# S5's tables in two buffer sets, a paced TensorE part and bias rows in pieces: one change to a four-layer hybrid kernel

## The chip, the cores and the metric

The kernel runs on one core of a Trainium2 chip. The metric is the device time of one execution in microseconds. A core has five engines that run side by side: TensorE (PE in the profile, with its weight loads as PEld), VectorE (DVE), ScalarE (ACT), GpSimd (POOL), and SyncE (SP), which here only issues DMA transfers. TensorE's clock has two levels, 1.2 and 2.4 GHz; the profile gives the granted clock of a stretch as a share of the higher one.

## The reference, cut to what matters

Four layers work on 256 tokens of width 1024 in float32. Each layer is half a SwiGLU FFN of width 2816, a mixer, and half an FFN again. The mixers are S5, HGRN2, gated DeltaNet and MoBA. The first layer's mixer, S5, holds 64 groups of 16 channels with 64 complex states each:

```
lam_bar = exp(lam * dt);  b_bar = ((lam_bar - 1) / lam) * (b_re + i b_im)
bu = einsum('blgh,gph->lbgp', u, b_bar)
h  = associative_scan: h[l] = lam_bar * h[l-1] + bu[l]
y  = real(einsum('lbgp,ghp->blgh', h, c)) + d_skip * u
x  = x + val * sigmoid(gate),   val, gate = split(gelu(y) @ w_glu)
```

The last layer's mixer, MoBA, is causal attention here (256 tokens are one block). A relative position bias of 32 buckets and 8 heads is added to its logits.

## The kernel before, in words

A FFN is worked off in units. A unit is two blocks of 128 rows of a weight matrix by 512 columns. For each unit SP loads the raw weights (L69, four raw buffers), ScalarE rounds them to a high part (L86), VectorE subtracts to get the low part (L87), and TensorE makes 12 matmuls of 128x512, three for each of two blocks and two token halves (L343 to L345). Four high and four low buffers let the split run four units ahead (`Weights.HL`). A FFN has 44 units of gate and up and then 22 of down. Every four units the hidden part h is transposed by TensorE (L435), then split too (L438, L439). After the last units the residual x is updated (L480) and transposed for the next stage (L226).

S5 needs tables that depend on its parameters alone: an inward table (`s5_in`), an outward table (`s5_out`), the kernel inside a chunk of eight tokens (`s5_k`), and powers of the rotation (`turn`, `s5_phases`). The generator `s5_prep` makes them beside the first FFN. It is advanced by `step`, which the FFN calls after each unit: at units 5, 7, ... 31, and then at each unit to 59. Its order is: loads of the parameters; transposes; exponentials and sines on VectorE; copies of lambda powers to `s5_l` (L667, GpSimd); scaling of b (L687 to L691); copies to `back` (L705, GpSimd); then a loop over eight j of eight groups each. In the loop GpSimd makes two halves of the inward table (L728 to L730) into a buffer `e`; VectorE makes the outward table (L733, L734, L736) into another part of `e`, which is stored (L737); TensorE multiplies for `s5_k` (L742, 16 matmuls); TensorE transposes the two inward halves (L756, 4 each), ScalarE copies each to one staging buffer `et` (L757), and SP stores it (L758). There is one `e`, so the steps of j+1 wait for those of j. After the loop GpSimd makes the first set of phases (L768 on).

The stage S5 itself loads the tables (L800, eight transfers for each `s5_k` part; L804 for the others) into five buffers in turn. Its order is: inward products (L862), VectorE's scan of the first half, the own-chunk products (L878 by `own`), outward transposes and products (L951, L878), then the same for the second half. In the second half's scan GpSimd makes one of two products of the first rotation (L894), which VectorE adds (L900); GpSimd makes before it the second set of phases and the eight products `xr` (L939). TensorE then does matmuls on zeros (L249) at three places.

The framework puts the instructions of an engine in an order of its own, by program order and by when they seem ready; it may move one forward past others. `keep_in_program_order` holds an instruction behind all that its engine was given before. An engine's queue is worked off in order, so one that waits holds all behind it.

The bias for MoBA is prepared in the second FFN (`moba_bias`): 26 small copies on GpSimd make a row for each head, and one transfer on ScalarE's queue writes each row 128 times to DRAM (L1713).

Of the kernel before, what the change touches and what calls it, by code (L numbers as in the profile page):

```python
# [9 lines left out]
F32 = mybir.dt.float32  # L10
# [16 lines left out]
def as_ap(ap, offset, dims):  # L27
    return bass.AP(tensor=ap.tensor, offset=ap.offset + offset, ap=dims)
# [71 lines left out]
class Model:  # L100
# [483 lines left out]
    def s5_prep(self, pool):  # L584


        nc, I = self.nc, self.I
# [131 lines left out]
        v.tensor_reduce(self.s5_place, self.ident.rearrange("p (a t) -> p t a", t=8), op=OP.add, axis=mybir.AxisListType.X)  # L719
        for j in range(8):  # L720
            r = slice(8 * j, 8 * j + 8)

            rs = (slice(8 * j, 8 * j + 4), slice(8 * j + 4, 8 * j + 8))
            for h, eb in zip(rs, ebs):
                wh = [128, 4, 8, 16]
                pb = [back[:, n, h].unsqueeze(3).to_broadcast(wh) for n in range(2)]
# [10 lines left out]
            dma(as_ap(self.s5_out, j * 1024, [[8192, 128], [128, 8], [1, 128]]), eo)  # L737

            p = self.aux.tile([128, 512], F32, name="aux")
            for g in range(2):  # L740
                for q in range(4):
                    nc.tensor.matmul(p[q * 32:q * 32 + 32, g * 128:g * 128 + 128],  # L742
                                     b1[:, 8 * j + 2 * q:8 * j + 2 * q + 2].rearrange("p g h -> p (g h)"),
                                     eo[:, 2 * q + g], start=True, stop=True)
# [8 lines left out]
            for h, eb in zip(rs, ebs):  # L753
                p = self.aux.tile([128, 512], F32, name="aux")
                for g in range(4):
                    nc.tensor.transpose(p[:, g * 128:g * 128 + 128], eb[:, g], self.ident)  # L756
                nc.scalar.copy(et.rearrange("p g c -> p (g c)"), p)  # L757
                dma(as_ap(self.s5_in, h.start * 128, [[8192, 128], [128, 4], [1, 128]]), et)  # L758

        self.s5_turn = pool.tile([128, 2, 16, 32], F32, name="s5turn", tag="s5pw")  # L760
        yield from self.s5_phases(self.s5_turn, 0, pool)

    def s5_phases(self, turn, half, pool):

        eng = self.nc.gpsimd
        t2 = pool.tile([128, 2, 16, 8], F32, name="s5t2", tag="s5F")
# [13 lines left out]

    def s5_token(self, k):

        self.nc.vector.transpose(self.s5_u[:, k].rearrange("p g t h -> p t g h"),
                                 self.s5_x[:, k].rearrange("p (c t) -> p t c", t=8))

    def s5(self, i):
        nc = self.nc
# [3 lines left out]
        tags = ["s5" + c for c in "ABCDE"]  # L791

        def load(kind, part):

            tags.append(tags.pop(0))
            t = self.s5_pool.tile([128, 16, 128], F32, name="tab", tag=tags[-1])
            if kind == "t":

                for s in range(8):
                    nc.sync.dma_start(t[s * 16:s * 16 + 16],  # L800
                                      as_ap(self.s5_k, part * 16 * 3840 + (7 - s) * 16, [[240, 16], [3840, 16], [1, 128]]))
            else:
                src = self.s5_in if kind == "in" else self.s5_out
                nc.sync.dma_start(t, as_ap(src, part * 2048, [[8192, 128], [128, 16], [1, 128]]))  # L804
            return t.rearrange("p (j q g) c -> p j q g c", q=4, g=2)
# [890 lines left out]
    def moba_bias(self, pool):  # L1696
# [16 lines left out]
        nc.scalar.dma_start(self.bias_rows, row.rearrange("h (o s) -> h o s", o=1).to_broadcast([8, 128, 384]))  # L1713

    def moba(self, i):
# [3 lines left out]
        with self.tc.tile_pool(name="moba", bufs=1) as pool, self.tc.tile_pool(name="moba2", bufs=2) as two:  # L1719
            bt = pool.tile([128, H, L], F32, name="bt")  # L1720
            if self.bias is not None:
                self.bias(pool)
# [96 lines left out]
```

## Time and profile before

| | us |
|---|---|
| median of 3 runs | 2225.79 (2224.76 to 2226.97) |
| the profiled execution: time, and span of its instructions | 2227.23, 2225.5 |
| TensorE matmul busy | 2142.0 (96%) |
| VectorE, ScalarE, GpSimd busy | 1452.5, 1159.0, 207.8 |
| granted TensorE clock, mean | 0.982 |

The profiled execution is one run under the hardware profiler; the difference of its time and its span is what lies around the program. Times within a trace count from the first instruction. Busy TensorE is no measure of useful work, as matmuls overlap and last longer at the lower clock. The first FFN ends near 245 us, S5 is from there to some 320 us, and the second FFN begins there.

### The profile page before, as it was taken

The numbers are of one execution on the slowest core, as the hardware profiler recorded it, in microseconds if no ns is written. First come the engines' busy times: TensorE is split into PE (matmuls) and PEld (weight loads), VectorE is DVE, ScalarE is ACT, GpSimd is POOL, SyncE is SP. The second block draws the span as 40 slices with busy tenths as digits, with TensorE's granted clock in tenths as the row PEclk, the third lists the DMA queues.
The fourth block names the chain that finished last, engine by engine and source line by source line (L and its number), as shares of the span: only waits on it lengthen the run. The fifth ranks groups of instructions, "written<-read, shape, count | busy, mean of one in ns | idle before, by whom it ended". The sixth has DMA issues, their size and how long they took to land.

```text
span 2225.5 us, 30259 instructions
## 1 busy us (share of the span) xinstructions
PE 2142.0 (96%) x11480; PEld 1768.3 (79%) x11480; DVE 1452.5 (65%) x2445; ACT 1159.0 (52%) x1876; POOL 207.8 (9%) x272
## 2 busy tenths in 40 slices
PE   8988888999999999999999999998999999999998
PEld 6766666888888888888788887787888888898886
DVE  7987674556555977555655788887555555666555
ACT  6434344445444855444544677764544544555443
POOL 0598600000000000001000000000000000000000
PEclk9999999999999999999999999999999999999999
DMA  8655966655555554655555543334555655655553
GB/s 252 191 193 200 250 184 161 205 175 191 186 189 190 171 168 136 189 178 189 176 180 176 163 141 105 105 115 131 175 186 180 199 182 187 199 162 170 189 180 105
DMA packets 317907, 389.64 MB, mean 175 GB/s; under 512 B 14192, under 2 KB 247856, under 8 KB 316736
## 3 DMA queue, kind: packets, MB, share of 16 engines
q1 hardware_dynamic: 314768, 383.92, 54.5%
q10 hardware_dynamic: 2800, 3.68, 0.9%
q8 instruction: 90, 1.47, 0.3%
q14 instruction: 57, 0.47, 0.1%
q0 software_dynamic: 192, 0.10, 0.0%
HBM read 375.65 MB, written 12.01 MB: 174 GB/s over the span
## 4 chain that ended last, share of the span: by engine, by line
PE 80%; ACT 5%; DVE 5%; issue 4%; DMA 3%; POOL 2%; SPq 0%; ACTq 0%; POOLq 0%; DVEq 0%
PE acc L343 23%; PE acc L345 23%; PE acc L344 23%; PE acc L311 2%; PE aux L435 2%; PE acc L312 2%; DVE lo L87 2%; PE acc L313 2%; ACT hi L86 1%; DMA raw<-in_ffn_w_up_dram 1%; ACT zb L1512 1%; PE aux L226 1%; POOL s5e L730 1%; POOL s5e L729 1%; POOL s5tmp L728 1%
## 5 line engine op out<-in xcount | busy, mean ns | idle before, releaser
L87 DVE TENSOR_TENSOR lo<-raw,hi 128x1024 fp32r<-128x1024 f32 x681 | 850.0, 1250 | 585.3 <-ACT hi L86 583.6
L86 ACT CAST hi<-raw 128x1024 fp32r<-128x1024 f32 x681 | 713.0, 1049 | 703.0 <-PE acc L345 648.0
L343 PE MATMUL acc<-hi,xhl 128*128 128x512 f32 x1568 | 625.7, 399 | 8.6 <-ACT hi L86 8.2
L344 PE MATMUL acc<-lo,xhl 128*128 128x512 f32 x1568 | 615.9, 393 | 2.4 <-DVE lo L87 2.3
L345 PE MATMUL acc<-hi,xhl 128*128 128x512 f32 x1568 | 615.3, 393 | 0.0
L343 PEld LDWEIGHTS acc<-hi,xhl 128*128 128x128 f32 x1568 | 296.1, 189 | 70.8 <-ACT hi L86 9.1
L345 PEld LDWEIGHTS acc<-hi,xhl 128*128 128x128 f32 x1568 | 296.0, 189 | 64.4 <-issue 0.9
L344 PEld LDWEIGHTS acc<-lo,xhl 128*128 128x128 f32 x1568 | 296.6, 189 | 63.6 <-DVE lo L87 5.1
L343 PE MATMUL acc<-hi,hhl 128*128 128x512 f32 x704 | 276.3, 392 | 0.0
L345 PE MATMUL acc<-hi,hhl 128*128 128x512 f32 x704 | 276.1, 392 | 0.0
L344 PE MATMUL acc<-lo,hhl 128*128 128x512 f32 x704 | 275.0, 391 | 0.0
L344 PEld LDWEIGHTS acc<-lo,hhl 128*128 128x128 f32 x704 | 132.5, 188 | 27.4
L345 PEld LDWEIGHTS acc<-hi,hhl 128*128 128x128 f32 x704 | 132.5, 188 | 27.4
L343 PEld LDWEIGHTS acc<-hi,hhl 128*128 128x128 f32 x704 | 132.6, 188 | 27.0
L313 PE MATMUL acc<-xhl,lo 128*128 128x256 f32 x520 | 150.0, 290 | 0.0
L311 PE MATMUL acc<-xhl,hi 128*128 128x256 f32 x520 | 149.7, 291 | 0.0
L312 PE MATMUL acc<-xhl,hi 128*128 128x256 f32 x520 | 148.4, 288 | 0.0
L423 ACT ACTIVATE sl<-acc,norm_r 128x256 f32<-128x256 f32 x176 | 83.6, 475 | 109.3 <-PE acc L345 88.6
L426 DVE TENSOR_TENSOR h<-acc,sl 128x256 f32<-128x256 f32 x176 | 74.0, 420 | 49.8 <-ACT sl L423 49.8
L313 PEld LDWEIGHTS acc<-xhl,lo 128*128 128x128 f32 x520 | 100.1, 193 | 2.0 <-DVE lo L87 1.0
L311 PEld LDWEIGHTS acc<-xhl,hi 128*128 128x128 f32 x520 | 99.7, 193 | 1.8 <-issue 0.9
L312 PEld LDWEIGHTS acc<-xhl,hi 128*128 128x128 f32 x520 | 99.9, 193 | 1.3 <-issue 1.1
(563 smaller groups left out, 2148.5 us busy)
## 6 DMA issues: line engine op xcount, KB each, us to landing
raw<-in_ffn_w_gate_dram SPq DMA_DIRECT2D x174, 512.0 KB, 3.8
raw<-in_ffn_w_up_dram SPq DMA_DIRECT2D x174, 512.0 KB, 4.8
raw<-in_ffn_w_down_dram SPq DMA_DIRECT2D x80, 1024.0 KB, 4.9
raw<-in_gdn_w_in_dram SPq DMA_DIRECT2D x24, 1024.0 KB, 5.2
raw<-in_hg_w_in_dram SPq DMA_DIRECT2D x16, 1024.0 KB, 5.4
raw<-in_moba_w_in_dram SPq DMA_DIRECT2D x12, 1024.0 KB, 5.1
raw<-in_ffn_w_down_dram SPq DMA_DIRECT2D x16, 512.0 KB, 3.7
raw<-in_s_w_glu_dram SPq DMA_DIRECT2D x16, 512.0 KB, 6.1
```

The source lines that it names most:

```text
L86: pin(self.nc.scalar.copy(hi, src))
L87: self.nc.vector.tensor_tensor(lo, src, hi.bitcast(F32), op=OP.subtract)
L226: nc.tensor.transpose(q[:, j * 128:j * 128 + 128], self.x[:, t, k * 128:k * 128 + 128], self.ident)
L311: t.matmul(p, hi, ah, start=first, stop=False)
L312: t.matmul(p, hi, al, start=False, stop=False)
L313: t.matmul(p, lo, ah, start=False, stop=last)
L343: mm(p, ah, hi[:, j], start=first and j == 0, stop=False)
L344: mm(p, ah, lo[:, j], start=False, stop=False)
L345: mm(p, al, hi[:, j], start=False, stop=last and j == n - 1)
L423: nc.scalar.activation(sl, p[:, :256], AF.Silu, scale=self.r_col[:, t:t + 1])
L426: return nc.vector.tensor_tensor(waiting[-1][1][:, t], p[:, 256:], sl, op=OP.mult)
L435: nc.tensor.transpose(q[:, c:c + 128], h[:, t, f * 128:f * 128 + 128], self.ident)
```

## The change

The table preparation gets a second buffer (`s5f`), so that j and j+1 write to different sets. TensorE's part of the loop is held in program order, and the transposes of j-1 (`turned`) come at the end of the turn of j. The generator is advanced at unit 2, at 6 to 9, at the even units to 18, and at each unit from 19 on; the loop takes 5 units for each of j = 0 to 3 and 4 for the others. The copies to `s5_l` and `back` go to ScalarE. At the end of the preparation, units 61 to 63, six tables are loaded, and the steps of the first phases stand between them; S5 has six table buffers for five. The bias rows are written by 32 transfers instead of one, one for each unit of the second FFN from unit 6 on.

```
             steps = [0]
+            bias = None
+            if self.prep is None and self.bias is not None:
+                bias = self.bias(pool)
+                self.bias = None
...
-                if self.prep is not None and n > 4:
-                    for _ in range(n % 2 if n < 32 else 1 if n < 60 else 0):
-                        next(self.prep, None)
+                if bias is not None and n > 4:
+                    next(bias, None)
+                if self.prep is not None and (n == 2 or 5 < n < 10 or n > 9 and n % 2 == 0 or n > 18):
+                    next(self.prep, None)
...
-            if self.prep is None and self.bias is not None:
-                self.bias(pool)
-                self.bias = None
...
-                    nc.gpsimd.tensor_copy(self.s5_l[q * 32:q * 32 + 32, n].rearrange("p (j g a) -> p j g a", j=8, g=2)[:, :, :, a],
+                    nc.scalar.copy(self.s5_l[q * 32:q * 32 + 32, n].rearrange("p (j g a) -> p j g a", j=8, g=2)[:, :, :, a],
...
-            nc.gpsimd.tensor_copy(back[:, :, :, n], pw[:, :, :, 8 - n])
+            nc.scalar.copy(back[:, :, :, n], pw[:, :, :, 8 - n])
         e = pool.tile([128, 16, 128], F32, name="s5e", tag="s5C")
-        eo, ebs = e[:, :8], (e[:, 8:12], e[:, 12:16])
+        more = pool.tile([128, 16, 128], F32, name="s5f", tag="s5G")
+        eos = e[:, :8], more[:, :8]
+        ebs = [(t[:, 8:12], t[:, 12:16]) for t in (e, more)]
...
+        pin = self.tc.keep_in_program_order
+        def turned(j):
+            for n, eb in enumerate(ebs[j % 2]):
+                p = self.aux.tile([128, 512], F32, name="aux")
+                for g in range(4):
+                    pin(nc.tensor.transpose(p[:, g * 128:g * 128 + 128], eb[:, g], self.ident))
+                nc.scalar.copy(et.rearrange("p g c -> p (g c)"), p)
+                dma(as_ap(self.s5_in, (8 * j + 4 * n) * 128, [[8192, 128], [128, 4], [1, 128]]), et)
...
             dma(as_ap(self.s5_out, j * 1024, [[8192, 128], [128, 8], [1, 128]]), eo)
+            yield
...
-                    nc.tensor.matmul(p[q * 32:q * 32 + 32, g * 128:g * 128 + 128],
+                    pin(nc.tensor.matmul(p[q * 32:q * 32 + 32, g * 128:g * 128 + 128],
...
             yield
-            for h, eb in zip(rs, ebs):
-                p = self.aux.tile([128, 512], F32, name="aux")
...
-                dma(as_ap(self.s5_in, h.start * 128, [[8192, 128], [128, 4], [1, 128]]), et)
+            if j < 4:
+                yield
+            if j:
+                turned(j - 1)
+            yield
+        turned(7)
+        self.s5_tags = ["s5" + c for c in "ABCDEG"]
+        self.s5_tabs = []
         self.s5_turn = pool.tile([128, 2, 16, 32], F32, name="s5turn", tag="s5pw")
-        yield from self.s5_phases(self.s5_turn, 0, pool)
+        phases = self.s5_phases(self.s5_turn, 0, pool)
+        for kind, part in (("in", 0), ("in", 1), ("in", 2), ("in", 3), ("t", 0), ("t", 1)):
+            self.s5_tabs.append(self.s5_load(kind, part))
+            next(phases, None)
+            if part % 2:
+                yield
...
-        nc.scalar.dma_start(self.bias_rows, row.rearrange("h (o s) -> h o s", o=1).to_broadcast([8, 128, 384]))
+        for k in range(0, 128, 4):
+            yield
+            self.tc.keep_in_program_order(nc.scalar.dma_start(
+                as_ap(self.bias_rows, k * 384, [[128 * 384, 8], [384, 4], [1, 384]]),
+                row.rearrange("h (o s) -> h o s", o=1).to_broadcast([8, 4, 384])))
```

`s5_load` is the former `load` of S5, with the six tags; S5's `load` takes the six tables from `s5_tabs` first and calls `s5_load` for the rest.

## Rows read from the trace of the kernel before

**Rows 1.** A stretch of the first FFN: length, busy us of each engine, clock, DMA.
```profile
114.00:172.80 58.80, 47.56 (x278) 36.43 (x277) 49.07 (x34) 21.95 (x34) 54.82 (x31) 0.91 0.56 192
```
**Rows 2.** Waits of TensorE to 330 us: total, times, longest.
```profile
PE acc L878 <- DMA tab<-s_k: 11.9, 3, 5.0
PE aux L756 <- POOL s5e L730: 11.2, 5, 3.5
PE aux L742 <- DVE s5e L736: 6.2, 3, 3.2
```
**Rows 3.** Timeline of TensorE, both FFNs: start us, duration us, instruction.
```profile
114.00 0.60 PE L435 MATMUL aux<-ident,h 128*128 128x128 f32 x4
...
120.03 0.64 PE L742 MATMUL aux<-s5e,s5D 128*32 128x128 f32 x16
...
123.50 1.04 PE L756 MATMUL aux<-ident,s5e 128*128 128x128 f32 x8
...
244.74 0.66 PE L226 MATMUL aux<-ident,x 128*128 128x128 f32 x4 [0.21 <-DVE x L480]
...
356.80 0.60 PE L435 MATMUL aux<-ident,h 128*128 128x128 f32 x4
...
368.18 0.60 PE L435 MATMUL aux<-ident,h 128*128 128x128 f32 x4
...
389.85 0.60 PE L435 MATMUL aux<-ident,h 128*128 128x128 f32 x4
```
**Rows 4.** The loop's three GpSimd lines: ns minimum, median, maximum; first and last start.
```profile
L728 POOL TENSOR_TENSOR s5tmp<-s5D,s5kk x16: 1058/1917/1925, 109.6 to 200.2; 128x512 f32<-128x512 f32 x16
...
L729 POOL TENSOR_TENSOR s5e<-s5D,s5kk x16: 1047/1916/2040, 110.6 to 195.9; 128x512 f32<-128x512 f32 x16
...
L730 POOL TENSOR_TENSOR s5e<-s5e,s5tmp x16: 1269/2140/2357, 113.7 to 202.2; 128x512 f32<-128x512 f32 x16
```
**Rows 5.** Groups of VectorE in 110 to 205 us: busy, mean ns, idle before.
```profile
L87 DVE TENSOR_TENSOR lo<-raw,hi 128x1024 fp32r<-128x1024 f32 x22 | 40.5, 1842 | 14.3 <-ACT hi L86 14.3
L734 DVE TENSOR_TENSOR s5e<-s5E,s5pw 128x1024 f32<-128x1024 f32 x7 | 12.8, 1829 | 1.0 <-DMA s_out<-s5e 0.8 <-PE aux L742 0.3
```
**Rows 6.** Timeline of VectorE before GpSimd's loop.
```profile
87.25 1.22 DVE L87 TENSOR_TENSOR lo<-raw,hi 128x1024 fp32r<-128x1024 f32 x1
```
**Rows 7.** Timeline of GpSimd.
```profile
86.00 12.20 POOL L667 COPY s5l<-s5small 32x16 f32<-32x16 f32 x16 [9.42 <-DVE s5small L510]
...
204.29 0.12 POOL L768 MEMSET s5turn<- 128x16 f32 x1
...
229.73 0.43 POOL L500 TENSOR_TENSOR s5turn<-s5t 128x112 f32<-128x112 f32 x1
243.99 0.13 POOL L768 MEMSET turn<- 128x16 f32 x1 [13.83 <-PE acc L345]
...
278.05 2.49 POOL L894 TENSOR_TENSOR tb<-inc,turn 128x512 f32<-128x512 f32 x2
```
**Rows 8.** Timelines of VectorE and TensorE at the end of S5's second scan.
```profile
280.57 1.29 DVE L900 TENSOR_TENSOR inc<-S,tb 128x512 f32<-128x512 f32 x2 [7.17 <-POOL tb L894]
...
288.03 1.31 DVE L948 STREAM_TRANSPOSE sc<-S 128x512 f32<-128x512 f32 x2
...
290.38 1.22 PE L951 MATMUL aux<-ident,sc 128*128 128x128 f32 x8
```
**Rows 9.** Issues of transfers: KB each, median us to landing.
```profile
s_in<-s5tmp SPq DMA_DIRECT2D x16, 256.0 KB, 3.8
```
**Rows 10.** Timeline of ScalarE and its queue in the second FFN.
```profile
348.66 0.79 ACTq L1713 DMA_DIRECT2D bias_rows<-row  x1
...
382.73 1.04 ACT L86 CAST hi<-raw 128x1024 fp32r<-128x1024 f32 x1 [15.60 <-DMA raw<-in_ffn_w_up_dram]
```
**Rows 11.** Two stretches of the second FFN, columns as in rows 1 (last: GB/s).
```profile
370.00:375.00 5.00, 5.00 (x23) 4.13 (x22) 0.00 (x0) 0.00 (x0) 0.00 (x0) 1.00 0.51 84
385.00:390.00 5.00, 4.91 (x13) 3.85 (x14) 3.89 (x7) 3.03 (x5) 0.00 (x0) 0.53 0.99 336
```

More of the change, by code (lines that the diff above doesn't have):

```diff
@@ L719, in s5_prep @@
         v.tensor_reduce(self.s5_place, self.ident.rearrange("p (a t) -> p t a", t=8), op=OP.add, axis=mybir.AxisListType.X)
+        pin = self.tc.keep_in_program_order
[6 more added lines that the diff above has]
+                dma(as_ap(self.s5_in, (8 * j + 4 * n) * 128, [[8192, 128], [128, 4], [1, 128]]), et)
         for j in range(8):
             r = slice(8 * j, 8 * j + 8)
-            rs = (slice(8 * j, 8 * j + 4), slice(8 * j + 4, 8 * j + 8))
-            for h, eb in zip(rs, ebs):
+            eo = eos[j % 2]
+            for n, eb in enumerate(ebs[j % 2]):
+                h = slice(8 * j + 4 * n, 8 * j + 4 * n + 4)
                 wh = [128, 4, 8, 16]
-                pb = [back[:, n, h].unsqueeze(3).to_broadcast(wh) for n in range(2)]
+                pb = [back[:, m, h].unsqueeze(3).to_broadcast(wh) for m in range(2)]
                 g = nc.gpsimd.tensor_tensor
@@ L741, in s5_prep @@
                 for q in range(4):
-                    nc.tensor.matmul(p[q * 32:q * 32 + 32, g * 128:g * 128 + 128],
-                                     b1[:, 8 * j + 2 * q:8 * j + 2 * q + 2].rearrange("p g h -> p (g h)"),
-                                     eo[:, 2 * q + g], start=True, stop=True)
+                    pin(nc.tensor.matmul(p[q * 32:q * 32 + 32, g * 128:g * 128 + 128],
+                                         b1[:, 8 * j + 2 * q:8 * j + 2 * q + 2].rearrange("p g h -> p (g h)"),
+                                         eo[:, 2 * q + g], start=True, stop=True))
             nc.scalar.copy(kk[:, j % 4].rearrange("p g c -> p (g c)"), p[:, :256])
@@ L752, in s5_prep @@
             yield
-            for h, eb in zip(rs, ebs):
-                p = self.aux.tile([128, 512], F32, name="aux")
-                for g in range(4):
-                    nc.tensor.transpose(p[:, g * 128:g * 128 + 128], eb[:, g], self.ident)
-                nc.scalar.copy(et.rearrange("p g c -> p (g c)"), p)
-                dma(as_ap(self.s5_in, h.start * 128, [[8192, 128], [128, 4], [1, 128]]), et)
-        self.s5_turn = pool.tile([128, 2, 16, 32], F32, name="s5turn", tag="s5pw")
-        yield from self.s5_phases(self.s5_turn, 0, pool)
+            if j < 4:
[6 more added lines that the diff above has]
+        self.s5_tabs = []
+        self.s5_turn = pool.tile([128, 2, 16, 32], F32, name="s5turn", tag="s5pw")
+        phases = self.s5_phases(self.s5_turn, 0, pool)
[4 more added lines that the diff above has]
+                yield
     def s5_phases(self, turn, half, pool):
         eng = self.nc.gpsimd
-        t2 = pool.tile([128, 2, 16, 8], F32, name="s5t2", tag="s5F")
+        t2 = self.s5_pool.tile([128, 2, 16, 8], F32, name="s5t2", tag="s5F")
         pin = self.tc.keep_in_program_order
@@ L779, in s5_phases, with s5_load @@
             yield
+    def s5_load(self, kind, part):
+        tags = self.s5_tags
+        tags.append(tags.pop(0))
+        t = self.s5_pool.tile([128, 16, 128], F32, name="tab", tag=tags[-1])
+        if kind == "t":
+            for s in range(8):
+                self.nc.sync.dma_start(t[s * 16:s * 16 + 16],
+                                       as_ap(self.s5_k, part * 16 * 3840 + (7 - s) * 16, [[240, 16], [3840, 16], [1, 128]]))
+        else:
+            src = self.s5_in if kind == "in" else self.s5_out
+            self.nc.sync.dma_start(t, as_ap(src, part * 2048, [[8192, 128], [128, 16], [1, 128]]))
+        return t.rearrange("p (j q g) c -> p j q g c", q=4, g=2)
     def s5_token(self, k):
@@ L790, in s5 @@
         pin = self.tc.keep_in_program_order
-        tags = ["s5" + c for c in "ABCDE"]
+        tags = self.s5_tags
         def load(kind, part):
[L795 to L805, printed above, removed]
+            if self.s5_tabs:
+                return self.s5_tabs.pop(0)
+            return self.s5_load(kind, part)
         with ExitStack() as ctx:
@@ L1721, in moba @@
             if self.bias is not None:
-                self.bias(pool)
+                self.settle(self.bias(pool))
             nc.scalar.dma_start(bt, as_ap(self.bias_rows, 127, [[383, 128], [128 * 384, H], [1, L]]))
```

## The prediction

> **What bounds the kernel now.** I read the table of stretches first, then TensorE's list of waits, then the timelines of the engines that these name. E below is the moment of the last transpose of the first FFN, 244.74 us [rows 3]. In 114.0 to 172.8 TensorE is busy for 47.56 of 58.80 us at a granted clock of 0.91, while GpSimd is busy for 54.82 [rows 1]: here the first FFN is held up by S5's table preparation, which runs beside it. The list of waits has three large items: the transposes of the inward table wait 11.2 us for GpSimd (L730), the small products (L742) 6.2 us for VectorE, and S5's own products 11.9 us for loads of its tables [rows 2].
>
> How much of that is on the path? Four units and one transposition of h take 368.18 - 356.80 = 11.38 us where nothing disturbs them [rows 3]; with 0.45 us for the transposition (an estimate, below its 0.60 because matmuls overlap), a unit is 2.73 us. After the transposition at 114.00, 33 of the 66 units are left. They need 33 x 2.73 = 90.1; three more transpositions 1.4; eight groups of L742 at 0.64 make 5.1; sixteen halves of L756 at 0.52 make 8.3; the turning of x about 1.2 [rows 3]. That is 106.1 us, and 130.7 pass. So 24.6 us are lost: 17.4 of them are the two waits, and the rest is the clock that falls behind them [rows 1, 2].
>
> The S5 stage is another matter. Its waits for tables look large, but the last step that releases the end of S5 is VectorE at L900, which waits 7.17 us for GpSimd (L894, begun at 278.05) [rows 7, 8]. VectorE ends its scan at 289.3, and TensorE transposes at 290.38: the late table costs about 1.1 us there, not 11.9.
>
> **The change part by part: the first FFN.** The preparation begins at unit 2 instead of 5. The loop over eight j begins at unit 25 instead of 34, with 5 units for each of j = 0 to 3 and 4 for the others. TensorE's part of j is pinned behind it: L742 two calls after j's VectorE part begins, the transposes of j-1 at the end of j's turn. GpSimd may start j when the transposes of j-2 have freed its buffer, and has until the end of the turn of j+1. Four units with L742 and two halves are 10.9 + 0.64 + 1.04 = 12.6 us. GpSimd's three instructions take per half 1.06 + 1.05 + 1.27 = 3.4 us at best and 1.92 + 1.92 + 2.14 = 6.0 at the median [rows 4], so 6.8 to 12.0 per j. Even the upper end is inside 12.6 and has most of a further turn to spare; only the last j has just the five units 57 to 61, 15.3 us. So both waits and the clock that falls with them should go: -24.6 us.
>
> What takes their place is VectorE. A low part (L87) takes 1.22 us without GpSimd beside it [rows 6], 1.84 on the mean in 110 to 205, where 42 such two-input operations and GpSimd's 48 stand together (22 of L87 and 20 of the three table operations, of which one row stands) [rows 5]. Undisturbed these would be 42 x 1.22 = 51 and 16 x 3.4 = 54, together 105 us of work in 95: the two overlap by a factor of at least 1.1. After the change, units 33 to 61 take TensorE 28 x 2.73 + 1.4 + 3.8 + 6.2 = 87.8 us. In them lie 28 low parts and about 18 table operations, 56 us, and six j of GpSimd, 41: 97 us. At a factor of 1.1 that just fits, one after the other it costs 9 us. Lower bound 0, upper 10; I take +5, the middle, since the four split buffers hold some of it.
> The Trainium skill, "SBUF — State Buffer", section "Who interferes with whom", speaks against this part: a VectorE operation with two SBUF inputs and a GpSimd operation that reads SBUF exclude each other for the whole instruction. By it these 97 us would stand in 87.8, and my sum would be 4 us longer. The measured 105 us in 95 say that it doesn't hold to the full here.
>
> **Copies on ScalarE.** The 24 copies of L667 leave GpSimd, where the last 16 take 12.2 us and hold everything behind them [rows 7], and 8 more at L705. So GpSimd's loop can start some 20 us sooner. No row shows such a copy on ScalarE. From below, 128 of the 1024 elements of its cast of 1.04 us [rows 10] make 0.13; from above, GpSimd's own 12.2 / 16 = 0.76. So 4 to 24 us, over some 11 units; I take 0.3, nearer the ScalarE row, 10 us. Even at 24 ScalarE would fall 10 us behind its casts, and the four split buffers hold 4 x 2.73 = 11. I cost the copies at nothing; without that cover it is up to 10 us. Each pair of inward transposes shares one staging buffer, so the second copy waits for the first's store, 3.8 us [rows 9]; the casts are queued behind it, and TensorE behind those after four units. In a turn of 12.6 us ScalarE then has four casts, 4.2, six operations of at most half a cast's elements, estimated at 0.6 each, 3.6, and this 3.8: 11.6, just covered. Uncovered it would be up to 4 us per j; I leave that to the second rival.
>
> **Six early loads and phases.** They move four one-piece loads and 16 small ones on SP from S5's stage to units 61 to 63, past S5's weight loads. SP can hold there until the last inward store has landed (2 x 3.8 us plus the copies); behind it stand weights for products some 50 us after E, so I cost this at nothing; without that cover it is 8 us. The first turn's phases move too. Before, GpSimd makes them from 204.29 to 230.16, long before E, and starts the second set at 243.99 [rows 7]. Now the first set stands behind j = 7, which waits for the transposes at unit 56. From there GpSimd needs 0.5 + 6.8 to 12.0 + 25.9 = 33.2 to 38.4 us; TensorE reaches E after 10 units, L742, two pairs of halves, the x turning and 0.8 us of evacuation: 27.3 + 0.6 + 2.1 + 1.2 + 0.8 = 32.0. So the second set starts 1.2 to 6.4 us after E, where it now starts 0.75 before. Behind it, as now, come the eight products for xr and then L894: 278.05 - 243.99 = 34.1 us [rows 7]. So the step that VectorE waits for at L900 comes 2.0 to 7.2 us later, measured from E; I take 4, the lower half, as GpSimd meets fewer VectorE operations late in the FFN. The tables are early now, which gives the 1.1 us. S5: +3, between +1 and +6.
>
> **Bias rows in 32 pieces.** One transfer of 1536 KB is issued at 348.66, and until ScalarE gets its weights again at 382.73, after 15.60 us of waiting [rows 10], 34 us pass. In 370 to 375 the core moves 84 GB/s, in 385 to 390 it moves 336 [rows 11]. From the transposition at 368.18 to the next, 389.85, 21.67 us pass instead of 11.38 [rows 3]: 10.3 us lost, the half clock afterwards in it. Thirty-two pieces, one a unit, are each 1/32 of these 34 us, so about 1.1 us in 2.73. At 84 GB/s for 1.1 us and 336 for 1.63 that is 234 GB/s on the mean, and a unit needs 0.52 MB in 2.73 us, 192: enough. ScalarE issues 32 times: the one issue was 0.79 us [rows 10], 0.3 to 0.8 each. A unit holds 1.04 for the cast and about 0.4 for the rest, below 2.73 in either case. Nothing. So -10.3; bounds -10.3 and 0.
> The Trainium skill, "DMA: Bandwidth & Descriptors", section "Bandwidth", speaks against pieces: transfers under 64 KB are dominated by their descriptors, and a MiB or more is advised. These are 48 KB. No one waits for them before the last layer, so by it too the sum would stay unless their packets cost the weights more than one transfer's do.
>
> **Sum.** -24.6 + 5 + 3 - 10.3 = -26.9 us. The profiled execution, span 2225.5 and time 2227.23, would be 2198.6 and 2200.3. The median of the runs is 1.4 below that time, 2225.79, so **2199 us**. A change under 0.2%, 4.5 us, can't be told from none.
>
> **Rivals.** (1) The forecast, 2193 to 2206: 0.58. (2) VectorE and GpSimd exclude each other, or the store wait reaches TensorE in one or two j: 10 instead of 5 in the FFN, GpSimd late by the full 6 in S5, some clock lost again, +3: -24.6 + 10 + 6 + 3 - 10.3 = -16, 2210. For it: VectorE at 49 of 58.8 us [rows 1]; against: the 105 in 95. 0.16. By the page on SBUF that is named above, the first half of this is the case. (3) Nothing is given back: the port fits, GpSimd is done by E, S5 gains the 1.1: -36, 2190. For it: 1.1 is what the trace shows; against: j = 7 can't start before unit 56. 0.15. (4) The pieces disturb the weights as the one did: -16.6, 2209; for it: 234 against 192 is no wide margin, and no row shows a piece. 0.05. (5) The other side: pinned, TensorE waits for GpSimd in every j, where now the scheduler's order may let a unit pass. It decides when a j takes over 12.6 us; to be slower by 0.2% it must lose 31 us in eight, a j of about 16.5. The median instructions give 12.0. 0.04. That the tables land earlier and change nothing is part of (1) already. The remaining 0.02 are for a loss that cancels the gain within 0.2%.
> The range 2187 to 2213 holds (1) to (4) with their bounds. Faster 0.94, same 0.02, slower 0.04.
>
> **What would show it.** Right: the L756 and L742 waits are gone from TensorE's list, the clock is at 1.00 from 114 to E, E falls at 220 to 230; transpositions of h stay 11.4 apart through the second FFN; ScalarE no longer waits 15 us there. S5's waits for tables are small, yet L900 still waits for GpSimd, and the time from E to the last pair of S5's outward transposes (290.38, now 45.6 us) is longer by 1 to 6 [rows 3, 8]. Wrong: TensorE waiting for L87 between units 33 and 61 by over 10 us; new PE waits behind L730; a shorter S5 stage, which would mean that GpSimd's phases were not last.

## The result, and the profile after

The changed kernel takes 2206.47 us (median of 4 runs, 2204.64 to 2208.11) against 2225.28 (2221.11 to 2226.97): ratio 0.9918, 95% interval 0.9901 to 0.9935, some 19 us faster. The forecast was 2199, with 2187 to 2213 as its range. So sign and range hold, but 19 us came where 27 were expected, and they came from other places than the sum says.

The profiled execution took 2208.11 us, its span is 2206.4. Beside the span of before, 2225.5, the 19.1 us split up as follows, by the same marks in both traces:
- until the last transposition of the first FFN (E): 239.28 instead of 244.74, -5.5 us;
- from E to the first transposition of h in the second FFN: 112.21 instead of 112.06, +0.15; in it S5, from E to its last pair of outward transposes, 46.62 instead of 45.64, +1.0;
- from there to the first transposition of h in the third FFN: 187.25 instead of 197.29, -10.0: the bias;
- all behind that: 1667.7 instead of 1671.4, -3.7. No edit works there. Below, a kernel whose instructions differ from the changed one's only in a buffer of S5's loop shows 1664.2 there, so this is difference from run to run.

The marks in the traces, first of the changed kernel (E, the second FFN, the third), then of the kernel before (the third):

```profile
239.28 0.63 PE L226 MATMUL aux<-ident,x 128*128 128x128 f32 x4 [1.04 <-ACT size L865]
...
351.49 0.60 PE L435 MATMUL aux<-ident,h 128*128 128x128 f32 x4
...
538.74 0.60 PE L435 MATMUL aux<-ident,h 128*128 128x128 f32 x4
```
```profile
554.09 0.60 PE L435 MATMUL aux<-ident,h 128*128 128x128 f32 x4
```

Of the signs that the prediction named, the waits of L756 and L742 are gone and so is ScalarE's wait of 15 us. Three others failed: E is not at 220 to 230, the clock is at 0.82 from 94.64 to 131.7 instead of 1.00 from 114 on, and S5's waits for tables are as large as before.

TensorE's waits up to 330 us, of the changed kernel (total, times, longest), answer to [rows 2]; L731 is the line of the inward transposes now, L759 that of the small products, L908 that of S5's own products:

```profile
PE aux L435 <- DVE h L426: 13.5, 6, 4.3
PE acc L908 <- DMA tab<-s_k: 12.2, 3, 6.4
```

L756's and L742's waits, 17.4 us together, are gone. In their place stands a wait that was 1.4 us before: the transposition of h (L435) waits 13.5 us for VectorE. Three stretches say where. The first row is of the kernel before, the others of the changed kernel (length, busy us of PE, PEld, DVE, ACT, POOL, clock, DMA share, GB/s):

```profile
78.00:114.00 36.00, 34.54 (x156) 28.25 (x157) 30.99 (x43) 16.96 (x22) 27.14 (x30) 1.00 0.62 191
```
```profile
78.00:131.70 53.70, 41.17 (x194) 32.03 (x192) 47.75 (x45) 23.21 (x49) 31.56 (x15) 0.87 0.47 154
131.70:239.30 107.60, 106.49 (x588) 85.77 (x587) 74.23 (x64) 54.56 (x86) 80.59 (x91) 1.00 0.71 234
```

From the transposition at unit 21 to that at unit 33, 35.9 us passed before (78.1 to 114.0), and 52.9 pass now (78.84 to 131.7). From unit 33 to E the new kernel is all but perfect: 107.6 us where the prediction worked out 106.1 for the bare work, TensorE busy for 106.49, the clock at 1.00. Before, that part took 130.7. So the removed waits gave their 23 us, and 17 were lost ahead of them. TensorE and VectorE there, in the changed kernel:

```profile
78.84 0.60 PE L435 MATMUL aux<-ident,h 128*128 128x128 f32 x4
94.64 0.33 PE L435 MATMUL aux<-ident,h 128*128 128x128 f32 x1 [4.27 <-DVE h L426]
98.84 0.90 PE L435 MATMUL aux<-ident,h 128*128 128x128 f32 x3 [3.61 <-DVE h L426]
113.30 0.33 PE L435 MATMUL aux<-ident,h 128*128 128x128 f32 x1 [1.00 <-DVE h L426]
117.51 0.90 PE L435 MATMUL aux<-ident,h 128*128 128x128 f32 x3 [3.65 <-DVE h L426]
```
```profile
85.69 3.44 DVE L693 TENSOR_TENSOR s5D<-s5D,s5tmp 128x1024 f32<-128x1024 f32 x1
89.06 1.21 DVE L87 TENSOR_TENSOR lo<-raw,hi 128x1024 fp32r<-128x1024 f32 x1
90.19 2.07 DVE L749 TENSOR_TENSOR s5tmp<-s5E,s5pw 128x1024 f32<-128x1024 f32 x1
92.19 2.07 DVE L87 TENSOR_TENSOR lo<-raw,hi 128x1024 fp32r<-128x1024 f32 x1
94.18 0.41 DVE L426 TENSOR_TENSOR h<-acc,sl 128x256 f32<-128x256 f32 x1
94.51 1.74 DVE L752 TENSOR_TENSOR s5e<-s5e,s5tmp 128x1024 f32<-128x1024 f32 x1
96.18 2.28 DVE L87 TENSOR_TENSOR lo<-raw,hi 128x1024 fp32r<-128x1024 f32 x1
98.38 0.41 DVE L426 TENSOR_TENSOR h<-acc,sl 128x256 f32<-128x256 f32 x1
```

The two halves of h (L426, 0.41 us each) stand 4.2 us apart on VectorE, behind low parts and table operations that take 1.7 to 2.3 us each instead of 1.22 [rows 6]. GpSimd runs beside them without a pause, and then stands still for 19.56 us:

```profile
84.77 3.29 POOL L693 TENSOR_TENSOR s5D<-s5D,s5tmp 128x1024 f32<-128x1024 f32 x1
...
114.12 1.92 POOL L744 TENSOR_TENSOR s5tmp<-s5D,s5kk 128x512 f32<-128x512 f32 x1
135.59 1.26 POOL L745 TENSOR_TENSOR s5e<-s5D,s5kk 128x512 f32<-128x512 f32 x1 [19.56 <-PE aux L731]
```

From 89.31 to 116.04, 26.73 us, VectorE has 12 of its large operations whole and parts of two, 16.2 us of work at 1.22, and GpSimd 13, 14.6 at the least durations of [rows 4]: 30.8 in 26.73, a factor of 1.15. VectorE is busy in every microsecond of it, so the stretching goes straight to TensorE.

Stretching is not all. Of VectorE's operations of 128x1024 with two inputs, 19 start between these two transpositions in the trace of before, 26.2 us together, and 25 in that of the changed kernel, 44.4 us. So 6 more of them stand there, 7.3 us at 1.22, and 10.9 us are added stretching. Of the 25, 10 are table operations, of the 19 only 3. The framework drew some ahead: VectorE ends the outward tables of j = 0, 1 and 2 (L752 at 94.51, 102.97 and 113.17) before the transposition at unit 33, while the program has j = 2 at unit 35.

The end of S5, of the changed kernel (VectorE, then TensorE), beside [rows 8]:

```profile
275.37 1.29 DVE L930 TENSOR_TENSOR inc<-S,tb 128x512 f32<-128x512 f32 x2 [6.50 <-POOL tb L924]
```
```profile
280.65 1.93 PE L908 MATMUL acc<-tab,ut 128*32 128x128 f32 x32 [6.44 <-DMA tab<-s_k]
282.92 3.19 PE L249 MATMUL aux<-zero 128*128 128x512 bf16 x7 [0.33 <-issue]
285.90 1.18 PE L981 MATMUL aux<-ident,sc 128*128 128x128 f32 x8
```

Nothing moved here: GpSimd is waited for 6.50 us (7.17 before), the last table part comes as late against E as before, and only two of TensorE's steps lie between it and the last transposes. VectorE's own last step is done at 284.1 (L978, 282.83 and 1.30 us long), 1.8 us before them. In the second FFN (window of the changed kernel, columns as above) TensorE doesn't stop, the clock is full, and no wait of ScalarE for weights is left of the 15.60 us in [rows 10]. Two transpositions of h come 13.6 and 12.8 us behind the one before instead of 11.4, with 58 and 54 matmuls of the products between them instead of 48, and two later ones 9.8 and 9.4; no time is lost by that:

```profile
340.00:391.00 51.00, 51.00 (x234) 41.87 (x233) 29.96 (x50) 26.25 (x36) 4.07 (x26) 1.00 0.63 197
```

### The profile page after: what moved, and what is told of

Read it like the earlier page. It is cut to its first block, busy times and chain, and to the rows that moved or that the text cites. A ratio compares the mean times of both kernels' runs of the same rounds, so it can differ in the third digit from the quotient of the medians.

```text
span 2206.4 us, 30282 instructions
## 1 busy us (share of the span) xinstructions
PE 2133.5 (97%) x11477; PEld 1763.2 (80%) x11480; DVE 1447.2 (66%) x2445; ACT 1165.6 (53%) x1908; POOL 186.0 (8%) x240
## 4 chain that ended last, share of the span: by engine, by line
PE 82%; DVE 6%; ACT 5%; issue 4%; DMA 2%; SPq 1%; POOL 0%; ACTq 0%; POOLq 0%; DVEq 0%
PE acc L343 23%; PE acc L345 23%; PE acc L344 23%; DVE lo L87 2%; PE acc L311 2%; PE acc L312 2%; PE aux L435 2%; PE acc L313 2%; ACT hi L86 1%; DMA tab<-s_k 1%; ACT zb L1542 1%; PE aux L226 1%; DMA raw<-in_s_w_glu_dram 0%; PE aux L249 0%; DVE cy L1419 0%
## 5 line engine op out<-in xcount | busy, mean ns | idle before, releaser
L87 DVE TENSOR_TENSOR lo<-raw,hi 128x1024 fp32r<-128x1024 f32 x681 | 847.9, 1247 | 543.4 <-ACT hi L86 540.2
L426 DVE TENSOR_TENSOR h<-acc,sl 128x256 f32<-128x256 f32 x176 | 74.0, 420 | 59.5 <-ACT sl L423 57.5
```

Source lines behind the costliest of these rows:

```text
L87: self.nc.vector.tensor_tensor(lo, src, hi.bitcast(F32), op=OP.subtract)
L426: return nc.vector.tensor_tensor(waiting[-1][1][:, t], p[:, 256:], sl, op=OP.mult)
```

## The experiments

What had to be told apart is the new loss in units 21 to 33. Theory A: VectorE and GpSimd hold each other up there, with VectorE's in-order queue carrying it to h. Rival B: ScalarE's copies hold the casts. Rival C: the earlier, denser preparation is too much for VectorE by itself. Then the two terms on which the forecast and the traces differ: S5 and the early loads; and the bias alone. "E to L981" below is the time from E to S5's last outward transposes, whatever line number these have in a run. Each ratio is to the kernel before, run beside it. The expectations of the later runs count E from the fourth matmul of its transposition, 0.4 us later than here. Their 22 us of waits at L435 in 60 to 135 are 12.8 on TensorE alone.

**1. VectorE's table operations pinned** (the two products likewise).
```diff
-v.tensor_tensor(split(eo), split(eo), ta, op=OP.add)
+pin(v.tensor_tensor(split(eo), split(eo), ta, op=OP.add))
```


> After the change, with VectorE's three operations of each table (L749, L750, L752) pinned to their place in the program as well. Theory A (the loss of some 18 us in units 21 to 33 of the first FFN comes from VectorE's in-order queue: table operations of j = 0 to 2, drawn ahead by the scheduler and stretched by GpSimd's loop, stand in front of the halves of h): TensorE's waits at L435 for h fall from some 22 us to under 8, E falls from 239.3 to 222-230, the time to 2190-2200. Rival B (ScalarE's 32 small copies hold back the casts that VectorE needs): the copies stay where they are, so E stays at 236-242 and the time at 2203-2209. Rival C (the earlier and denser preparation is simply too much work for VectorE in these units, whatever its order): the waits at L435 stay or move a few units on, E 234-242.

Measured: 2225.92, ratio 1.001 (0.9997 to 1.0022); E 250.90, E to L981 50.9. L435's waits fell to 7.7 us, and units 21 to 33 take 43.8 us instead of 52.9. But from there to E it is 128.6 instead of 107.6, as TensorE now waits for the tables:

```profile
PE aux L759 <- DVE s5f L752: 6.1, 3, 2.2
PE aux L759 <- DVE s5e L752: 3.6, 2, 2.1
```

All three theories missed E and the time. Before unit 33 the run bears out the second half of theory A: with 6 table operations there instead of 10, 9 of the 17 us are gone, though GpSimd still stretches what is left. But with the table operations at their program's place, the pinned products behind them wait, and all of the gain is gone later on. In this kernel, with TensorE's part pinned, VectorE's tables have to come ahead of their program order.

**2. The 32 copies back on GpSimd** (the 24 of L669 likewise).
```diff
-nc.scalar.copy(back[:, :, :, n], pw[:, :, :, 8 - n])
+nc.gpsimd.tensor_copy(back[:, :, :, n], pw[:, :, :, 8 - n])
```


> After the change, with the 32 small copies (L669, L707) back on GpSimd. GpSimd's loop then starts some 18 us later. Theory A: VectorE's table operations of j = 0 to 2 no longer meet GpSimd's, so the waits at L435 for h in 60 to 135 fall by a part (from 22 us to 8-16), and some of it comes back as waits for GpSimd at L731; E 232-242. Rival B (the copies hold ScalarE's casts): the waits at L435 vanish, E 222-230, the time 2190-2200. Rival C: nothing changes before unit 33, E 238 or later, and GpSimd is late for L731: the time 2206-2215.

Measured: 2203.53, ratio 0.9903 (0.9888 to 0.9918); E 234.29, E to L981 46.3. VectorE and GpSimd of this run:

```profile
83.46 1.22 DVE L87 TENSOR_TENSOR lo<-raw,hi 128x1024 fp32r<-128x1024 f32 x1
84.59 1.22 DVE L693 TENSOR_TENSOR s5D<-s5D,s5tmp 128x1024 f32<-128x1024 f32 x1
```
```profile
81.61 13.11 POOL L669 COPY s5l<-s5small 32x16 f32<-32x16 f32 x16 [12.36 <-DVE s5small L512]
94.80 1.94 POOL L692 TENSOR_TENSOR s5D<-s5D,s5small 128x1024 f32<-128x1024 f32 x1
96.82 3.25 POOL L693 TENSOR_TENSOR s5D<-s5D,s5tmp 128x1024 f32<-128x1024 f32 x1
```

As theory A had it: L693 takes 1.22 us instead of 3.44 and the next turn (the transposition of h) comes 11.4 us later (79.14 to 90.52) instead of 15.8. Units 21 to 33 take 43.1 us instead of 52.9; from there to E it is 112.1 instead of 107.6. The waits for GpSimd at L731 that the theory expected did not come. The run also takes the copies off ScalarE, so it alone doesn't tell theory A from rival B; run 4 does. GpSimd's 13 us of small copies don't stretch VectorE at all. They had kept GpSimd's heavy operations away from VectorE in a stretch where VectorE has nothing to spare; the change took that distance away.

**3. GpSimd's loop on a quarter of the data, and (4) its scaling of b too** (the last two lines, for all three operations).
```diff
-wh = [128, 4, 8, 16]
+wh = [128, 1, 8, 16]
...
+q = slice(0, 16)
+nc.gpsimd.tensor_tensor(t1[:, q], b1[:, q], fw[1][:, q], op=OP.mult)
```


> After the change, with GpSimd's three operations of the loop (L744 to L746) done on one of each four groups; this leaves out three quarters of the inward table. VectorE's work, the stores and TensorE's transposes stay. Theory A has two parts, order and contention: with GpSimd's work cut to about a quarter, L87 should fall from 2.0-2.3 to about 1.3 us in units 21 to 33. If contention is the larger part, the waits at L435 fall from 22 us to under 6 and E to 222-228; if order is the larger part they fall only to 10-16 and E to 230-236. Rivals B and C (ScalarE's copies; VectorE's own work): E stays within 3 us of 239.3. In S5, GpSimd's phases can begin some 6 us earlier, which would show whether L930's wait of 6.5 us for GpSimd shrinks and what then ends last: by the trace the tables do, within 2 us, so E to the last transpose L981 should stay at 44.5-46.6.

> As the kernel with GpSimd's loop on one of each four groups, and GpSimd's three operations before the loop (L691 to L693 on b1 and b2) on a quarter as well; this leaves out three quarters of the inward table and of the scaled matrix that goes into it. Theory A, contention: VectorE's L693 (3.43 us beside GpSimd's) and the L87 before it (2.65) fall to about 1.3, the turn-to-turn time of units 21 to 25 falls from 15.3 to 11.4-13, and E from 230.6 to 222-228. Rival B (ScalarE's copies hold sl and the casts, 5.5 us of them in 81 to 88): that turn stays at 14.5-16 and E at 229-232.

Measured: (3) 2196.26, ratio 0.9876 (0.9863 to 0.9888), E 230.25; (4) 2192.06, ratio 0.9854 (0.9823 to 0.9884), E 225.87. TensorE of run 4:

```profile
78.49 0.60 PE L435 MATMUL aux<-ident,h 128*128 128x128 f32 x4
89.87 0.27 PE L435 MATMUL aux<-ident,h 128*128 128x128 f32 x1
92.83 0.55 PE L435 MATMUL aux<-ident,h 128*128 128x128 f32 x3 [2.46 <-DVE h L426]
106.37 0.72 PE L435 MATMUL aux<-ident,h 128*128 128x128 f32 x4
118.71 0.60 PE L435 MATMUL aux<-ident,h 128*128 128x128 f32 x4
```

Taking three quarters of GpSimd's work away (zeros stand in the rest) brings E forward by 9.0 and then 13.4 us. The second is inside what theory A gave for it (222 to 228). The first is between its two cases: the waits at L435 are 6.0 us, as if contention were the larger part, and E is where it was to be if order were. In run 4 units 21 to 33 take 40.2 us instead of 52.9. From unit 33 to E both runs need 107.2 us, and the changed kernel 107.6: there the same cut of GpSimd's work brings nothing. ScalarE's copies are where they were, and the first turn is 11.4 us long with them: rival B falls. From before's 35.9 to 40.2 some 4 us remain, with VectorE busy for 35.20 of 40.22: that much is left for rival C and for what GpSimd still does. Of the 4.4 us that run 4's E is ahead of run 3's, nearly nothing is left behind S5, whose E to L981 is 44.5 in run 3 and 48.4 in run 4: the first transposition of h in the second FFN comes at 340.32 and 340.11.

**5. The loop five units later.**
```diff
-if self.prep is not None and (n == 2 or 5 < n < 10 or n > 9 and n % 2 == 0 or n > 18):
+if self.prep is not None and (n == 2 or 5 < n < 10 or n > 9 and n % 2 == 0 or n > 28):
...
-            if j < 4:
-                yield
```


> After the change, with the preparation called at every second unit up to 28 instead of 18 and four units for each j: the loop begins about unit 30 instead of 25 and ends about where it did. Rival C (too much work at once in units 21 to 33, where GpSimd's first two j run together with VectorE's): the waits at L435 in 60 to 135 fall from 22 us with TensorE's pipeline counted twice (12.8 on TensorE alone) to under 6, E to 226-234, the time to 2196-2204. Theory A as a fixed bill (each pair of a VectorE and a GpSimd operation costs about a microsecond, wherever it stands): the waits move to units 30 to 40, E 236-241, the time 2203-2210.

Measured: 2209.01, ratio 0.9940 (0.9918 to 0.9961), E 239.92, E to L981 47.5. The turn at unit 33 comes 6.8 us sooner (124.9 instead of 131.7), and all of it is lost again between 185 and 210, where VectorE (24.36 of 25 us busy just before) is late with the residual x and TensorE waits 5.4 us for it (L226 for L482):

```profile
160.00:185.00 25.00, 25.00 (x146) 20.35 (x139) 24.36 (x16) 10.30 (x14) 22.22 (x13) 1.00 0.68 207
185.00:210.00 25.00, 19.57 (x113) 15.24 (x113) 20.61 (x16) 11.49 (x23) 15.47 (x8) 0.86 0.71 234
```

So it is a bill that moves with the work, and costs time only where VectorE has no slack. E and the time are what theory A gave; the place, near the end of the FFN and not units 30 to 40, is not.

**6, 7. One set of inward buffers.** In the first try the transposes of j-1 stand behind GpSimd's operations of j in the program, so that the single set adds no wait and the transposes take the next j's values. The order of work on every engine is that of the changed kernel but for the buffer's name and one GpSimd operation, and the run serves as its repeat: 2208.01, ratio 0.9926 (0.9899 to 0.9954), E 239.55, but E to L981 44.4 instead of 46.6. The second try (the lines below the gap) puts the transposes at the head of j.
```diff
-ebs = [(t[:, 8:12], t[:, 12:16]) for t in (e, more)]
+ebs = [(t[:, 8:12], t[:, 12:16]) for t in (e, e)]
...
+            if j:
+                turned(j - 1)
```


> After the change, with the inward table's GpSimd buffers in one set instead of two (the outward buffers stay in two). GpSimd can begin j only when TensorE has turned j-1, so it can't run j = 0 and 1 in one go in 89 to 116. If the two sets matter, TensorE waits at L731 for 5 to 10 us at the last j, GpSimd's phases begin later against E, S5 grows by 3 to 8 us and the time is 2206-2216, though the waits at L435 after 95 us may halve. If the spreading matters more, E is 232-238 and the time 2200-2206.

> After the change, with one set of inward buffers, and the transposes of j-1 put ahead of GpSimd's operations of j (in the run one_set they stood behind them, so that the one set made no wait and the transposes took the next j's values). Now GpSimd really begins j only when TensorE has turned j-1, at the start of j's turn, and has one turn of 12.6 us for it, where it needs 6.8 to 12.0. Theory A (port contention where VectorE has no slack): GpSimd's busy time in 95 to 115 falls from 19.6 us to about 12, the turns of units 25 to 33 come to 14-16 us apart instead of 18.5, E 232-236, the time 2198-2204. Rival (the two sets are needed): TensorE waits for GpSimd at L731 in several j, 1 to 4 us each, E 240-250, the time 2207-2217.

Measured, run 7: 2204.04, ratio 0.9912 (0.9899 to 0.9926), E 233.14, E to L981 47.3. GpSimd's busy time from 95 to 115 is 7.89 us instead of 19.61, the turn at unit 33 comes at 124.8, and L435 waits 10.3 us instead of 13.5; the two turns from unit 25 on take 17.5 and 13.1 us, where theory A had 14 to 16 each. TensorE never waits for GpSimd at L731. So the second set of inward buffers isn't what removed the waits of [rows 2]. Whether the pinned order did, or the second set of outward buffers, or the earlier start and the slower pace of the loop, no run takes apart. The 6.1 us that E gained turned into 2.4 us of time, which the intervals don't tell from none. S5 is longer now, and VectorE and TensorE show by what:

```profile
272.22 1.29 DVE L930 TENSOR_TENSOR inc<-S,tb 128x512 f32<-128x512 f32 x2 [8.69 <-POOL tb L924]
```
```profile
280.45 1.25 PE L981 MATMUL aux<-ident,sc 128*128 128x128 f32 x8 [3.58 <-DVE sc L978]
```

**8. The same with the copies back on GpSimd.** 

> The same with the 32 small copies back on GpSimd, which kept GpSimd from running beside VectorE's L693 and gave E 234.65 by itself. If the two gains add: E 229-233, the time 2195-2201, the fastest of the complete kernels. If GpSimd, with the copies, gets too late for the last j: TensorE waits for it at the end of the FFN, E 234-240 and S5 longer by 3 to 8 us, the time 2203-2212.

Measured: 2207.39, ratio 0.9930 (0.9916 to 0.9943), E 237.67, E to L981 47.3. The gains don't add: GpSimd, late by its copies, is waited for at L731 (4.5 us), and one turn takes 24.6 us (105.5 to 130.1).

**9. Without the six early loads.**
```diff
-for kind, part in (("in", 0), ("in", 1), ("in", 2), ("in", 3), ("t", 0), ("t", 1)):
-    self.s5_tabs.append(self.s5_load(kind, part))
+for n in range(6):
```


> After the change, without the six loads that were moved ahead of S5's stage (they are issued in the stage as before; the phases stay at units 61 to 63). By the trace the tables land no earlier with them than in the kernel before, so the time from E to the last L981 stays at 46-48 us and the whole within 2 us of the changed kernel's. If they do bring something, S5 is 1 to 4 us longer without them.

Measured: 2206.88, ratio 0.9925 (0.9897 to 0.9953), E 238.63, E to L981 44.1. The early loads bring nothing that can be seen, and SP's queue shows a reason: in the changed kernel the third and fourth inward loads stand behind the last inward store and are issued 2.1 us after E. Before, all four were issued 7 us ahead of E. SP of the changed kernel, then of before:

```profile
238.73 0.32 SPq L733 DMA_DIRECT2D s_in<-s5tmp  x1
...
241.38 0.81 SPq L817 DMA_DIRECT2D tab<-s_in  x2
```
```profile
235.83 1.82 SPq L804 DMA_DIRECT2D tab<-s_in  x2
```

Together with run 6 this run also says how much S5's length means: two kernels that differ in the buffer of a few operations alone show 46.6 and 44.4.

**10. The phases into GpSimd's gaps.**
```diff
+            for _ in range((0, 2, 1, 1, 1, 0, 1, 0)[j]):
+                next(phases, None)
...
+        for n, _ in enumerate(self.s5_phases(self.s5_turn2, 1, pool)):
+            if n % 2:
+                yield
```


> The kernel of the run paced_one_set, with GpSimd's work kept in program order and its phases moved: the first turn's phases in GpSimd's gaps between j = 1 and j = 4 (in a buffer of their own), the second turn's right behind j = 7 instead of behind the end of the FFN, and without the six early loads. In paced_one_set the step that VectorE waits for at L930 came 38.7 us after E, where the changed kernel has it 36.1 after E, and E to the last L981 took 47.9. Theory (with an earlier E, S5 is bound by GpSimd's phases, as the forecast's +3 had it): L930's wait for GpSimd falls from 8.7 to under 4 us, E to L981 comes to 43-45.5, and with E at 233-237 the time is 2198-2203. Rival (the tables and not GpSimd end S5): E to L981 stays at 45-48, or TensorE waits at L731 because the phases make GpSimd late, E 237-243: the time 2203-2210.

Measured: 2214.21, ratio 0.9964 (0.9953 to 0.9976), E 247.37, E to L981 45.6. The rival: GpSimd is now full (47.95 of 50 us busy in 160 to 210), TensorE waits 8.5 us for it at L731 and the clock falls to 0.90 in that stretch. What the run settles is S5. VectorE, then TensorE:

```profile
280.54 1.29 DVE L933 TENSOR_TENSOR inc<-S,tb 128x512 f32<-128x512 f32 x2 [1.16 <-POOL tb L927]
```
```profile
288.83 1.93 PE L911 MATMUL acc<-tab,ut 128*32 128x128 f32 x32 [4.77 <-DMA tab<-s_k]
```

The wait for GpSimd is down to 1.16 us and S5 is no shorter than before: the last part of `s_k` then ends it.

**11. Two units later, paced.**
```diff
-if self.prep is not None and (n == 2 or 5 < n < 10 or n > 9 and n % 2 == 0 or n > 18):
+if self.prep is not None and (n == 2 or 5 < n < 10 or n > 9 and n % 2 == 0 or n > 22):
...
-            if j < 4:
+            if j < 2:
```
on top of run 7. 

> The kernel of the run paced_one_set (E 233.5, its turns of units 21 to 33 at 78.4, 94.2, 111.7, 124.8), with the loop begun two units later: calls at every second unit up to 22 instead of 18, and five units only for j = 0 and 1. Theory: what is left of the loss before unit 33 is too much VectorE work at once; two units more to do it in take 2 to 5 us off E, 229-232, and if S5 grows by no more than 1 the time is 2199-2203, the fastest complete kernel. Rival (the loss moves to the end of the FFN, where the loop now has less room, as in the run later_loop): E 233-239, the time 2203-2209.

Measured: 2206.63, ratio 0.9925 (0.9912 to 0.9939), E 236.69, E to L981 48.1, with L981 waiting 7.6 us for VectorE. As in run 5 the loss only moved.

**12. The bias pieces alone, on the kernel before.**
```diff
+                if bias is not None and n > 4:
+                    next(bias, None)
...
+        for k in range(0, 128, 4):
+            yield
```


> The kernel before, with the bias rows alone written in 32 pieces, one a unit of the second FFN. Forecast of the bias term: -10.3 us, so 2213-2217 against 2225; transposes of h 11.4 apart through the second FFN but where VectorE's own work stretches one; no wait of 15 us on ScalarE. Rival (the pieces cost the weights as much as the one transfer): 2222-2226.

Measured: 2212.67 against 2223.94, ratio 0.9956 (0.9941 to 0.9970), 6.7 to 13.1 us. In the profile the second FFN, by the marks used above, takes 187.29 us (355.59 to 542.88), -10.0. Its first FFN and S5 are those of before, and they end at 245.84 instead of 244.74 and take 44.1 us instead of 45.6: so much they differ from one execution to the next.

## Why the prediction was right and where it failed

**The waits of L756 and L742, -24.6.** Right. From unit 33 to E the changed kernel needs 107.6 us instead of 130.7. The second set of inward buffers is not needed for it (run 7); that the pinned order does it is argued, not shown.

**VectorE and GpSimd, +5, bounds 0 to 10.** This is the step that failed, in place and in size. The sum counted units 33 to 61 only, 97 us of work in 87.8. There the loss is 1.5 us (107.6 against 106.1). What the change does to units 21 to 33 was given as a fact ("The loop over eight j begins at unit 25 instead of 34") and costed at nothing, and it cost 17.0: 52.9 us from the turn at unit 21 to that at unit 33, where before it was 35.9. The factor was well chosen (1.1 used, 1.15 measured); I applied it to the wrong stretch, and as a mean. Before, VectorE was busy for 30.99 of 36 us there, with GpSimd's heavy operations beside it for only 9.6. Now GpSimd's operations and six more of VectorE's own found no slack, while GpSimd's other 35 operations of the loop, after 131.7, cost next to nothing. Runs 3 and 4 show that without three quarters of GpSimd's work 13 of the 17 go, and run 1 that 9 of them go when fewer table operations stand ahead of h. These are two sides of one loss and do not add. Some 4 remain in run 4, which VectorE's own work explains by its busy time (argued, not shown). Part of the 17 is the clock, 0.87 on the mean: TensorE is idle for 12.5 of 53.7 us, and the rest is matmuls at the lower level behind the waits.
The rule that the prediction weighed, the Trainium skill's "SBUF — State Buffer", "Who interferes with whom", would have put the 30.8 us of work from 89.31 on in 30.8; it took 26.73. Its other half holds in the first FFN here: an operation with one input from SBUF is untouched, L426 stays at 0.41 to 0.43 us and L439 at 0.68 to 0.69 beside GpSimd.

**Copies on ScalarE, nothing.** The size was right: 0.20 us each at L669 and 0.44 at L707, where 0.3 was taken. The cover held too (run 4's first turn is 11.4 us). But the step "GpSimd's loop can start some 20 us sooner" was read as a gain, and it carried the loss: with the copies back, E is 5.0 us earlier (run 2).

**Early loads, nothing.** Right that they cost nothing (run 9). But the 1.1 us that S5 was to get from early tables didn't come: SP held, as the prediction said that it can, behind the last inward store, so that most of these loads weren't early and the tables don't land earlier.

**S5, +3, between +1 and +6.** Measured +1.0, but S5 took 44.1 to 46.6 us in three executions that differ little there (the changed kernel, runs 6 and 9), so no change can be told. Here the step that failed is a size: GpSimd's chain from the transposes at unit 56 (206.0) to the second set was to take 33.2 to 38.4 us and took 32.7, as the phases need 24.3 us and not 25.9 and j = 7 needs 7.7, and TensorE reached E 33.3 us after these transposes and not 32.0. GpSimd of the changed kernel, from j = 7 to the second set:

```profile
206.70 3.06 POOL L745 TENSOR_TENSOR s5f<-s5D,s5kk 128x512 f32<-128x512 f32 x2 [3.13 <-PE aux L731]
...
238.71 0.12 POOL L792 MEMSET turn<- 128x16 f32 x1
```

So the second set starts 0.57 us before E instead of 1.2 to 6.4 after it. An early E alone changes nothing in this, since both count from the same transposes: in run 2, with E at 234.29, it starts at 233.72, again 0.57 before. In run 7 the transposes that release j = 7 stand a unit later. There the second set starts at 236.75, 3.6 after E, and S5 ends on VectorE behind GpSimd at 47.3. In runs 5, 8 and 11 it starts 3.4 to 5.6 after E, and S5 takes 47.3 to 48.1. So the mechanism is real where j = 7 is late. And the prediction's view of S5 was half right: GpSimd's chain and the tables end within a microsecond or two of each other, so that taking away the wait at L930 alone brings nothing (run 10), and in run 4, where the second set starts 1.3 us before E, S5 still takes 48.4 with TensorE waiting 4.24 us for the last part of `s_k`.

**Bias pieces, -10.3.** Right: -10.0 in the changed kernel and alone. In the second FFN neither TensorE nor ScalarE waits for a transfer of weights. The pieces do not go out one a unit, as the program has them: ScalarE issues most of them in ones and threes (391.32, 391.63, 392.01).

So the 7.8 us between forecast and result add up as follows: the first FFN gave 14.1 less than expected (5.5 instead of 19.6) and the bias 0.3 less, S5's part came out 2.9 better than forecast, and 3.7 came behind the third FFN's start, where nothing was changed: 14.1 + 0.3 - 2.9 - 3.7 = 7.8. That the time lies inside the range owes something to luck: a loss of 17 us that no term and no rival of the prediction placed there was partly made good by the 2.9 and the 3.7, neither of them foreseen. The complete kernels tried here lie between 2203.5 and 2226; none is faster than the changed kernel by more than the intervals allow (0.9903 and 0.9912 against 0.9918).

## What to carry to other kernels

When work of one engine is brought forward, look at the slack of its neighbour in the stretch where it will now run, not only in the stretch that it leaves: GpSimd's operations cost some 13 us where VectorE had been 86% busy almost without them (30.99 of 36), and next to nothing where it is 69% busy with them (74.23 of 107.6). An engine's long, light duty (here 13 us of small copies) may be what keeps two heavy users of a resource apart; ask what moves up when it is taken away. And where two chains end a stage within a microsecond or two, price neither alone: the wait with the larger number vanished in run 10 and the stage kept its length.

## What the runs showed of the hardware

- Two-input operations on VectorE and GpSimd stretch each other to nearly the sum of their times: L87 (128x1024) on VectorE took 2.07 us and L744 (128x512) on GpSimd 1.92 side by side, where the least durations are 1.22 and 1.06. L693, 128x1024 on both, took 3.44 and 3.29; with GpSimd's cut to a quarter VectorE's took 1.76. GpSimd's copies of 32x16 (16 in 13.11 us) left VectorE's at 1.21 to 1.23.
- Thirty-two transfers of 48 KB, issued by ScalarE within 96 us in about 0.3 us each, cost the weights' loads nothing that shows; one transfer of the same 1536 KB had cost 10 us.
